# A two-layer encoder in split fp32: another lead-in, and weight splits held back at the heads of three feed-forwards

## The chip, the cores and the metric

The kernel runs on one core of one Trainium2 chip. The metric is device microseconds of that core from launch to end. Three runs of the kernel before took 1055.67, 1056.27 and 1058.92 us; the median, 1056.27, is the time before. Its engines are named as in the profile: PE (TensorE, matrix products), with PEld its weight loads, DVE (VectorE), ACT (ScalarE), POOL (GpSimd), and SP, whose queue issues the DMAs.

## The reference

x is 256 rows of 1024, float32. Two layers; each is a SwiGLU feed-forward with half weight, a mixer (a convolution module in the first layer, differential attention in the second), and another feed-forward. Each of these six sub-layers has a norm ahead and a norm behind:

```python
def _rmsnorm(x, g, eps=RMS_EPS):
    y = xf * lax.rsqrt(jnp.mean(xf * xf, axis=-1, keepdims=True) + eps)
    return (y * g.astype(jnp.float32)).astype(x.dtype)

def _half_ffn(x, g_pre, g_post, w_gate, w_up, w_down):
    h = _rmsnorm(x, g_pre)                      # w_gate, w_up: 1024 x 2816
    f = (jax.nn.silu(h @ w_gate) * (h @ w_up)) @ w_down
    return x + 0.5 * _rmsnorm(f, g_post)
```

## The kernel before

The six sub-layers are called a (feed-forward), b (convolution), c and d (feed-forwards), e (attention), f (feed-forward), and run in this order (the loop over `subs`, L762).

Products in float32 precision are made of three: every operand is split into a high part (rounded, `wh`, `xTh`, `hh`) and a low part (`wl`, `xTl`, `hl`: the operand less its high part), and `mm3` (L151) adds high x high, high x low and low x high in PSUM. So each weight is loaded as float32 (`raw`), ACT copies its high part (L113) and DVE subtracts for the low part (L114). The weights are jobs of 512 KB (128 partitions x 1024 numbers). There are 5 buffers for raw jobs and NW = 12 for split ones. `pump` (L119) issues load and split of the next jobs as long as fewer than 12 are ahead of the oldest not yet freed; `free` (L128) frees one and calls `pump`.

The 256 rows of x are two blocks of 128 (tb = 0, 1). `prenorm` (L181) squares a block on ACT (the tiles j), takes the mean and the power -1/2 on POOL, multiplies x by the gain and the norm on DVE (the tiles xn). `turn` (L209) then transposes the block on PE (the tiles pt) into xTh and xTl. `postnorm` (L219) does the like for the result of a sub-layer and adds it to x.

A feed-forward (`ffn`, L329) has 11 chunks of 256 columns of gate and up. A chunk of gate is two jobs (k 0 to 3 and 4 to 7 of the eight 128-row pieces), and so is one of up. The first two chunks (the lead) are done with x as the stationary operand (`proj_x`, L254): four tiles px, one for each block and chunk, each of 48 products with 256 columns, then silu on ACT (sx), the product on DVE (hx), and transposes of it on PE into the tiles ht (`flip`, L201; `hook_flips`, L205). So a tile can start before the second block is normed. In a the order of the tiles is `TURN` (both blocks of chunk 0, then of chunk 1), in c, d and f it is `TWO` (both chunks of block 0 first). From chunk 2 on, the main loop (`projs`, L273) makes the transposed result directly, 18 tiles gu, each with silu (sg), product (h) and split (hh, hl). `Down` (L287) adds the down products into four PSUM banks, that of tile kt after the gate and up products of tile kt + 1; those of the last 8 come at the end (`finish`, L315), block by block, so that the postnorm of block 0 lies beside the products of block 1.

Within an engine instructions run in the order that the scheduler of the framework sets. `tc.keep_in_program_order` and `after` (L73) fix it in places. All DMAs of the kernel are issued by SP, in order.

Of the kernel before, what the change touches and what calls it, by code (L numbers as in the profile page):

```python
# [35 lines left out]
NRAW = 5  # L36
NDV = 4
WARM = (16, 6, 6)


class _Side:
# [8 lines left out]
def trunk_kernel(  # L50
# [37 lines left out]
    warm = cp.tile([P, 1], F32, name="warm")  # L88
    ones_r = cp.tile([33, P], F32R, name="ones_r")
    A.activation(ones_r, ones_d[0:33, :], AF.Copy, scale=float(D))  # L90
    ones_e = cp.tile([P, 1], F32, name="ones_e")
    G.memset(ones_e, 1.0 / P)

# [10 lines left out]

    ready = {}

    def issue(i):
        src, shape = jobs[i]
        raw = rawp.tile([P, *shape], F32, tag="raw", name=f"raw{i}")
        nc.sync.dma_start(raw, src)  # L110
        hi = wp.tile([P, *shape], F32R, tag="wh", name=f"wh{i}")
        lo = wp.tile([P, *shape], F32R, tag="wl", name=f"wl{i}")
        A.copy(hi, raw)  # L113
        V.tensor_tensor(lo, raw, r32(hi), ALU.subtract)  # L114
        ready[i] = (hi, lo)

    issued, oldest, gone = [0], [0], set()

    def pump():  # L119
        while issued[0] < min(oldest[0] + NW, len(jobs)):  # L120
            issue(issued[0])
            issued[0] += 1

    def need(i):
        pump()
# [67 lines left out]
        pending.append(lambda: turn(tb, xn, name))  # L193

    pending, flips = [], []

    def hook():
        while pending:
# [55 lines left out]
    def proj_x(pairs, order, name):  # L254

        for n, (tb, i) in enumerate(order):
# [13 lines left out]
                hook()  # L270
            yield tb, i, ps

    def projs(pairs, name):  # L273

        for c, (w1, w2) in pairs:
            for f in range(2):
                ps = proj(w1, w2, f, f"{name}{2 * c + f}")
                if f:
                    w1.free()
                    w2.free()  # L280
                yield 2 * c + f, ps

    def split_to(hi, lo, src):
        A.copy(hi, src)
        V.tensor_tensor(lo, src, r32(hi), ALU.subtract)

    class Down:  # L287

# [35 lines left out]
                self.ws[kt].free()  # L324

    TWO = [(tb, i) for tb in range(NTB) for i in range(2)]
    TURN = [(tb, i) for i in range(2) for tb in range(NTB)]

    def ffn(hp, jb, name):  # L329
        dn = Down([w for r in jb for w in r[2]], TAIL, name)  # L330
        q = []

        def tiles(c):
# [6 lines left out]
        for tb, i, ps in proj_x([r[:2] for r in jb[:2]], TURN if name == "a" else TWO, name):  # L340
            sg = sp.tile([P, FC], F32, tag="sg", name=f"sx{name}{tb}{i}")
            A.activation(sg, ps[:, :FC], AF.Silu)
            h = sp.tile([P, FC], F32, tag="hf", name=f"hx{name}{tb}{i}")
            V.tensor_tensor(h, ps[:, FC:], sg, ALU.mult)
            for f in range(2):
                flip(turned[i][:, f, tb, :], h[:, f * P:(f + 1) * P])
        for kt, ps in projs([(c, jb[c][:2]) for c in range(2, len(jb))], name):
# [7 lines left out]
            A.activation(sg, ps[:, 0, :], AF.Silu)  # L355
# [272 lines left out]
    def attn(hp, name):  # L628
# [112 lines left out]


    subs = [
        ("a", lambda p: ffn(p, J00, "a"), ffn_norm_pre[0, 0], ffn_norm_post[0, 0], True, conv_params),
        ("b", lambda p: conv(p, "b"), mix_norm_pre[0], mix_norm_post[0], False, None),
        ("c", lambda p: ffn(p, J01, "c"), ffn_norm_pre[0, 1], ffn_norm_post[0, 1], True, None),
        ("d", lambda p: ffn(p, J10, "d"), ffn_norm_pre[1, 0], ffn_norm_post[1, 0], True, attn_params),
        ("e", lambda p: attn(p, "e"), mix_norm_pre[1], mix_norm_post[1], False, None),
        ("f", lambda p: ffn(p, J11, "f"), ffn_norm_pre[1, 1], ffn_norm_post[1, 1], True, None),
    ]  # L750
    nc.sync.dma_start(xs[0], x[0, 0:P, :])
    g = gain(subs[0][2], "prea")
    for n in range(2):
        issue(issued[0])
        issued[0] += 1
    nc.sync.dma_start(xs[1], x[0, P:S, :])
    with tc.high_priority():
        prenorm(0, g, "a")
        hook()
    prenorm(1, g, "a")  # L760
    for n, (name, body, _, post, half, also) in enumerate(subs):
        last = n == len(subs) - 1  # L762
        with tc.tile_pool(name=f"hp{name}", bufs=8) as hp:
            dn = body(hp)
            if also is not None:
                also()
            gpost = gain(post, f"post{name}")
            gpre = None if last else gain(subs[n + 1][2], f"pre{n + 1}")
            for tb in range(NTB):
                dn.finish(tb)  # L770
                with tc.high_priority():
                    postnorm(tb, dn.acc[tb], gpost, half, name, out[0] if last else None)
                    if not last:
                        prenorm(tb, gpre, subs[n + 1][0])
            dn.free()


# [29 lines left out]
```

## Time and profile before

| | |
|---|---|
| median of three runs | 1056.27 us |
| the profiled execution | 1059.09 us, its span 1057.4 us |
| PE busy | 1022.3 us, 97% |
| DVE, ACT, POOL busy | 659.4, 553.7, 72.4 us |
| mean granted clock of PE | 0.993 |
| read from HBM | 175.40 MB, 167 GB/s over the span |

The span runs from the first to the last instruction. A timeline's row has the start and the length of an instruction, or of several of one kind; in brackets stands how long the engine had been idle and what ended that. Products of PE overlap: a row of 0.28 us whose successor starts 0.12 us later took PE 0.12. The granted clock is in shares of 2.4 GHz; at the very start its column shows 1.00 while the products stand as far apart as at the lower level, so there the spacing is what to read.

### The profile page before, as it was taken

Reading aid. Unit: us, or ns where it says so; the run is one execution under the profiler, and the core shown is the slowest. Engines: PE = TensorE matmul, PEld = TensorE weight load, DVE = VectorE, ACT = ScalarE, POOL = GpSimd, SP = SyncE. Lnnn points to the kernel's source line nnn. Section 1 sums busy time; section 2 is a strip of 40 time slices with the busy share of each in tenths; the row PEclk is TensorE's granted clock in tenths of the full one; section 3 lists DMA queues with packets and bytes.
Section 4 is the critical chain, followed back from the end, with each engine's and each line's share of the span. In section 5 each row is a group of like instructions: output and inputs, shape, how many; then the busy total and the mean of one; then the engine's idle time right before and its main releaser. Section 6 shows DMA issues by size and latency. Waiting matters only on the chain.

```text
span 1057.4 us, 17903 instructions
## 1 busy us (share of the span) xinstructions
PE 1022.3 (97%) x7133; PEld 947.2 (90%) x7133; DVE 659.4 (62%) x1007; ACT 553.7 (52%) x933; POOL 72.4 (7%) x110
## 2 busy tenths in 40 slices
PE   6999999999979999999999999999999999999997
PEld 5999999899967989999989999998899789999995
DVE  6755556689996755545475555566778685555542
ACT  6564445476845644434455444454578665445431
POOL 1000000031460100000010000001001110000000
PEclk9999999999989999999999999999999999999999
DMA  9866465386000666465555564653843255664511
GB/s 297 284 210 223 152 199 181 111 267 197 4 1 1 226 205 223 149 215 180 160 181 178 182 224 153 199 182 125 283 148 101 80 168 185 191 215 158 185 58 40
DMA packets 130493, 177.62 MB, mean 168 GB/s; under 512 B 6174, under 2 KB 112710, under 8 KB 130409
## 3 DMA queue, kind: packets, MB, share of 16 engines
q1 hardware_dynamic: 130408, 176.47, 51.6%
q8 instruction: 56, 0.92, 0.3%
q14 instruction: 29, 0.23, 0.1%
HBM read 175.40 MB, written 1.05 MB: 167 GB/s over the span
## 4 chain that ended last, share of the span: by engine, by line
PE 78%; DVE 10%; DMA 4%; ACT 3%; issue 3%; POOL 2%; SPq 0%; DVEq 0%; POOLq 0%; ACTq 0%
DVE co L487 4%; PE gua L152 3%; PE gua L154 3%; PE gua L153 3%; PE guf L152 3%; PE guc L152 3%; PE guf L154 3%; PE guc L154 3%; PE gud L154 3%; PE guc L153 3%; PE gud L152 3%; PE gud L153 3%; PE guf L153 3%; DVE wl L114 2%; DMA raw<-in_ffn_w_gate_dram 2%
## 5 line engine op out<-in xcount | busy, mean ns | idle before, releaser
L114 DVE TENSOR_TENSOR wl<-raw,wh 128x1024 fp32r<-128x1024 f32 x320 | 389.1, 1223 | 134.4 <-ACT wh L113 132.1
L113 ACT CAST wh<-raw 128x1024 fp32r<-128x1024 f32 x320 | 333.7, 1051 | 137.5 <-PE accd L154 14.2
L152 PE MATMUL guf<-xTh,wh 128*128 128x256 f32 x288 | 82.1, 285 | 0.0
L152 PE MATMUL guc<-xTh,wh 128*128 128x256 f32 x288 | 82.1, 285 | 0.0
L152 PE MATMUL gua<-xTh,wh 128*128 128x256 f32 x288 | 82.1, 285 | 0.0
L154 PE MATMUL gua<-xTh,wl 128*128 128x256 f32 x288 | 81.7, 284 | 0.0
L154 PE MATMUL guf<-xTh,wl 128*128 128x256 f32 x288 | 81.7, 284 | 0.0
L154 PE MATMUL guc<-xTh,wl 128*128 128x256 f32 x288 | 81.7, 284 | 0.0
L152 PE MATMUL gud<-xTh,wh 128*128 128x256 f32 x288 | 81.2, 282 | 0.0
L154 PE MATMUL gud<-xTh,wl 128*128 128x256 f32 x288 | 81.1, 281 | 0.0
L153 PE MATMUL gud<-xTl,wh 128*128 128x256 f32 x288 | 81.1, 281 | 0.0
L153 PE MATMUL guc<-xTl,wh 128*128 128x256 f32 x288 | 81.0, 281 | 0.0
L153 PE MATMUL gua<-xTl,wh 128*128 128x256 f32 x288 | 81.0, 281 | 0.0
L153 PE MATMUL guf<-xTl,wh 128*128 128x256 f32 x288 | 81.0, 281 | 0.0
L487 DVE SCALAR_TENSOR_TENSOR co<-u,wdw,co 128x256 f32<-128x256 f32 x120 | 61.7, 578 | 0.0
L153 PEld LDWEIGHTS guc<-xTl,wh 128*128 128x128 f32 x288 | 54.7, 190 | 0.5
L153 PEld LDWEIGHTS guf<-xTl,wh 128*128 128x128 f32 x288 | 54.6, 190 | 0.5
L153 PEld LDWEIGHTS gua<-xTl,wh 128*128 128x128 f32 x288 | 54.6, 190 | 0.5
L152 PEld LDWEIGHTS guf<-xTh,wh 128*128 128x128 f32 x288 | 54.4, 189 | 0.5
L152 PEld LDWEIGHTS gua<-xTh,wh 128*128 128x128 f32 x288 | 54.4, 189 | 0.5
L152 PEld LDWEIGHTS guc<-xTh,wh 128*128 128x128 f32 x288 | 54.4, 189 | 0.5
L152 PEld LDWEIGHTS gud<-xTh,wh 128*128 128x128 f32 x288 | 54.2, 188 | 0.5
(357 smaller groups left out, 2670.3 us busy)
## 6 DMA issues: line engine op xcount, KB each, us to landing
raw<-in_ffn_w_gate_dram SPq DMA_DIRECT2D x88, 512.0 KB, 5.0
raw<-in_ffn_w_up_dram SPq DMA_DIRECT2D x88, 512.0 KB, 4.8
raw<-in_ffn_w_down_dram SPq DMA_DIRECT2D x88, 512.0 KB, 4.7
raw<-in_conv_w_pw_dram SPq DMA_DIRECT2D x24, 512.0 KB, 4.7
raw<-in_attn_w_qkv_dram SPq DMA_DIRECT2D x24, 512.0 KB, 4.8
raw<-in_attn_w_o_dram SPq DMA_DIRECT2D x8, 512.0 KB, 4.6
gpre<-in_ffn_norm_pre_dram SPq DMA_DIRECT2D x3, 512.0 KB
x<-in_x_dram SPq DMA_DIRECT2D x2, 512.0 KB
```

The lines of the kernel that those rows point to most:

```text
L113: A.copy(hi, raw)
L114: V.tensor_tensor(lo, raw, r32(hi), ALU.subtract)
L152: T.matmul(o, sh, mh, start=first, stop=False)
L153: T.matmul(o, sh, ml, start=False, stop=False)
L154: T.matmul(o, sl, mh, start=False, stop=last)
L487: tap[ct, t] = V.scalar_tensor_tensor(c, u[:, t:t + S], wdw[:, ct, t:t + 1], c, ALU.mult, ALU.add)
```

## The change

In the lead-in, `first_norm` replaces the broadcast load of the gain, the two `prenorm` and the two `turn` of a. It loads the gain as 8 rows of 128 and transposes it, transposes raw x, multiplies by the gain per partition out of PSUM (ya), and splits that into xTh and xTl. The norm rs, one number a row of x, is worked out later and applied to the products: as the scale of silu and a factor in the lead, and as two multiplications by `row` (rs along the columns) in the 18 tiles of the main loop of a. 24 products of 32 rows run on PE ahead of x (`WARM0`). A load of x or a weight waits for the last load but one (`in_turn`); the first six weights are split at places written out by hand.

`proj_jobs` does the lead of a weight by weight: both blocks of a tile for one job, then the next; in each the products with low x come before those with low weights. The second chunk's two tiles lie in banks of the down sums (`acc`). The second block of x is turned inside the first twelve products.

In c, d and f `hold` limits the jobs that may be issued to the first 8 of the feed-forward. `release` lets two more after the second tile, two after the third and all after the fourth, each behind the silu and product of that tile on ACT and DVE. The parameter loads are issued after the 17th weight load.

```diff
-    def issue(i):
-        src, shape = jobs[i]
-        raw = rawp.tile([P, *shape], F32, tag="raw", name=f"raw{i}")
-        nc.sync.dma_start(raw, src)
...
     def pump():
-        while issued[0] < min(oldest[0] + NW, len(jobs)):
-            issue(issued[0])
-            issued[0] += 1
+        while issued[0] < min(oldest[0] + NW, limit[0]):
+            i, raw, _ = fetch()
+            split_to(*slot(i), raw)
+
+    def hold(first, n=None):
+        limit[0] = len(jobs) if n is None else first + n
+
+    def release(upto, *done):
+        with ExitStack() as st:
+            for ins in done:
+                st.enter_context(after(ins))
+            limit[0] = len(jobs) if upto is None else upto
+            pump()
...
+    def first_norm(row):
...
+        for _ in range(WARM0):
+            for g in range(4):
+                q = slice(32 * g, 32 * g + 32)
+                pin(T.matmul(four[g][:, 0:S], ident_r[q, :], twice[q].to_broadcast([32, 2, P]),
+                             start=True, stop=True))
...
+            d = pin(nc.sync.dma_start(dst, src)) if dst is not None else pin(fetch_into(w))
+            if len(last) > 1:
+                tc.add_manual_dep(d.ins, last[-2].ins.name, mybir.DependencyInfo(
+                    mybir.DependencyClass.Sync, mybir.DependencyReason.DATA), reason="in_turn")
+            last.append(d)
...
+        pin(nc.sync.dma_start(gr, row.rearrange("(k p) -> k p", p=P)))
+        get(xs[0], x[0, 0:P, :])
+        get(None, None)
+        get(xs[1], x[0, P:S, :])
+        for _ in range(3):
+            get(None, None)
...
+        turned(0, 0, ps_acc, "acc")
+        turned(0, 1, ps_acc, "acc")
+        scaled(0, 0)
+        weight_high(0)
+        high(0, 0)
+        scaled(0, 1)
+        high(0, 1)
+        low(0, 0)
+        weight_low(0)
+        weight_high(1)
+
+        def second():
+            turned(1, 0, ps_mi, "mi")
+            scaled(1, 0)
+            high(1, 0)
+            low(0, 1)
+            low(1, 0)
+            weight_low(1)
+            weight_high(2)
...
+    def proj_jobs(pairs, name):
...
+                        for n, (s, v) in enumerate(((xTh, 0), (xTl, 0), (xTh, 1))):
+                            if first and n == 2:
+                                pending.pop(0)()
+                            for k in range(k0, k0 + w.per):
+                                pin(T.matmul(ps[:, m * FC:(m + 1) * FC], s[:, k, c], w(k)[v],
+                                             start=n + k == 0, stop=n == 2 and k == KD - 1))
...
+                r = late[:, tb:tb + 1]
+                sa = A.activation(sg, ps[:, :FC], AF.Silu, scale=r)
+                hv = V.scalar_tensor_tensor(h, ps[:, FC:], r, sg, ALU.mult, ALU.mult)
             for f in range(2):
                 flip(turned[i][:, f, tb, :], h[:, f * P:(f + 1) * P])
+            release((j0 + LEAD, j0 + LEAD + 2, j0 + LEAD + 4, None)[n] if late is None else
+                    (j0 + 6, j0 + 10, j0 + 12, None)[n], sa, hv)
...
+                V.tensor_tensor(sg, ps[:, 0, :], row, ALU.mult)
+                A.activation(sg, sg, AF.Silu)
+                V.tensor_tensor(sg, sg, row, ALU.mult)
...
-        prenorm(0, g, "a")
-        hook()
-    prenorm(1, g, "a")
+        late = first_norm(subs[0][2])
+    heads = [None] + [jb[0][0].ids[0] for jb in (J01, J10)] + [None, J11[0][0].ids[0]]
...
+            with after(fetched[LATER]):
+                if also is not None:
+                    also()
...
+            if not last:
+                if heads[n] is None:
+                    release(None)
+                else:
+                    hold(heads[n], LEAD)
             dn.free()
```

What stands where on three engines follows. In the names a number behind the letters is the job (wh0), the block and half (xnd10: block 1, half 0) or the block and chunk (pxd01).

On ACT at the start, before: the squares (ja) of block 0, two weights, then the copies of transposed x.

```order
L186 ACTIVATE ja00_123,ppa0_122<-x0_95 128x512
L186 ACTIVATE ja01_127,ppa0_122<-x0_95 128x512
L113 CAST wh0_111<-raw0_109 128x1024
L113 CAST wh1_117<-raw1_115 128x1024
L216 CAST xTh_97<-pta00_137 128x4x128
L186 ACTIVATE ja10_152,ppa1_151<-x1_96 128x512
L216 CAST xTh_97<-pta01_144 128x4x128
L186 ACTIVATE ja11_156,ppa1_151<-x1_96 128x512
L113 CAST wh2_178<-raw2_176 128x1024
```

After: the first weight stands ahead of the copies of x, each further weight ahead of a copy of the second block, and the squares come behind all of them.

```order
L95 CAST ident_r_93<-ident_79 128x128
L285 CAST wh0_167<-raw0_139 128x1024
L275 CAST xTh_99<-ya00_165 128x4x128
L275 CAST xTh_99<-ya01_171 128x4x128
L285 CAST wh1_176<-raw1_142 128x1024
L275 CAST xTh_99<-ya10_199 128x4x128
L285 CAST wh2_205<-raw2_144 128x1024
L275 CAST xTh_99<-ya11_217 128x4x128
L282 ACTIVATE ja00_222,parts0_152<-x0_97 128x512
```

The squares moved from the front to behind the fourth copy of x, and the copies wait for ya, not for the normed x.

On DVE at the head of d, where block 1 is normed, before:

```order
L114 TENSOR_TENSOR wl164_5962<-raw164_5959,wh164_5961 128x1024
L231 SCALAR_TENSOR_TENSOR x1_96<-ync10_5906,rsqc1_5916,x1_96 128x512
L231 SCALAR_TENSOR_TENSOR x1_96<-ync11_5910,rsqc1_5916,x1_96 128x512
L188 TENSOR_TENSOR xnd10_5923<-x1_96,gpre3_5763 128x512
L188 TENSOR_TENSOR xnd11_5927<-x1_96,gpre3_5763 128x512
L114 TENSOR_TENSOR wl165_5968<-raw165_5965,wh165_5967 128x1024
L161 TENSOR_SCALAR mspd1_5929<-ppd1_5920 128x1
L114 TENSOR_TENSOR wl166_5974<-raw166_5971,wh166_5973 128x1024
L192 TENSOR_SCALAR xnd10_5923<-xnd10_5923,rspd1_5931 128x512
L192 TENSOR_SCALAR xnd11_5927<-xnd11_5927,rspd1_5931 128x512
L114 TENSOR_TENSOR wl167_5980<-raw167_5977,wh167_5979 128x1024
L344 TENSOR_TENSOR hxd00_6044<-pxd00_5993,sxd00_6042 128x256
```

The jobs 164 to 167 are the ninth to twelfth of d. After, the same stretch:

```order
L370 SCALAR_TENSOR_TENSOR x1_98<-ync10_5972,rsqc1_5982,x1_98 128x512
L370 SCALAR_TENSOR_TENSOR x1_98<-ync11_5976,rsqc1_5982,x1_98 128x512
L210 TENSOR_TENSOR xnd10_5989<-x1_98,gpre3_5829 128x512
L210 TENSOR_TENSOR xnd11_5993<-x1_98,gpre3_5829 128x512
L183 TENSOR_SCALAR mspd1_5995<-ppd1_5986 128x1
L214 TENSOR_SCALAR xnd10_5989<-xnd10_5989,rspd1_5997 128x512
L214 TENSOR_SCALAR xnd11_5993<-xnd11_5993,rspd1_5997 128x512
L509 TENSOR_TENSOR hxd00_6081<-pxd00_6031,sxd00_6080 128x256
L356 TENSOR_TENSOR xTl_100<-ptd10_6120,xTh_99 128x4x128
L356 TENSOR_TENSOR xTl_100<-ptd11_6127,xTh_99 128x4x128
L509 TENSOR_TENSOR hxd01_6150<-pxd01_6084,sxd01_6149 128x256
L448 TENSOR_TENSOR wl164_6156<-raw164_6153,wh164_6155 128x1024
```

The four subtractions wl164 to wl167 moved from between the steps of the norm to behind hxd01, or later.

On PE in the second tile of d, before, where the transposes of the first hx (htd0) and of block 1 (ptd10) stand:

```order
L154 MATMUL pxd01_6046<-wh163_5955,xTl_98 128x256
L152 MATMUL pxd01_6046<-wh163_5955,xTh_97 128x256
L207 MATMUL htd0_5991<-ident_79,hxd00_6044 128x128 x2
L213 MATMUL ptd10_6082<-ident_79,xnd10_5923 128x128 x4
L153 MATMUL pxd01_6046<-wl163_5956,xTh_97 128x256
L154 MATMUL pxd01_6046<-wh163_5955,xTl_98 128x256
```

After:

```order
L176 MATMUL pxd01_6084<-wh161_6009,xTl_100 128x256
L346 MATMUL htd0_6029<-ident_79,hxd00_6081 128x128 x2
L174 MATMUL pxd01_6084<-wh162_6015,xTh_99 128x256
L175 MATMUL pxd01_6084<-wl162_6016,xTh_99 128x256
L176 MATMUL pxd01_6084<-wh162_6015,xTl_100 128x256
```

The transposes of hx moved from behind the 40th to behind the 24th product of that tile; those of block 1 come nine products later.

## Rows read from the trace of the kernel before

**Rows 1.** The page, busy time of each engine, its share of the span, instructions.
```profile
PE 1022.3 (97%) x7133; PEld 947.2 (90%) x7133; DVE 659.4 (62%) x1007; ACT 553.7 (52%) x933; POOL 72.4 (7%) x110
```

**Rows 2.** Waits of PE, by what ended them: us, times, longest.
```profile
PE htd L207 <- DVE hxd L344: 2.7, 2, 2.4
PE hta L207 <- DVE hxa L344: 1.4, 1, 1.4
...
PE htc L207 <- DVE hxc L344: 1.2, 2, 0.9
PE htf L207 <- DVE hxf L344: 1.1, 2, 1.0
```

**Rows 3.** Timeline of the lead-in: start, length, engine, line, what, count [idle before].
```profile
0.80 0.38 SPq L751 DMA_DIRECT2D x<-in_x_dram  x1
...
4.50 0.63 ACT L186 ACTIVATE ja<-x 128x512 bf16<-128x512 f32 x1 [2.10 <-DMA x<-in_x_dram]
...
8.21 1.05 ACT L113 CAST wh<-raw 128x1024 fp32r<-128x1024 f32 x1 [2.23 <-DMA raw<-in_ffn_w_gate_dram]
...
8.37 1.97 PE L213 MATMUL pta<-ident,xna 128*128 128x128 f32 x8 [8.37 <-DVE xna L192]
...
9.70 1.05 ACT L113 CAST wh<-raw 128x1024 fp32r<-128x1024 f32 x1 [0.45 <-DMA raw<-in_ffn_w_gate_dram]
...
11.29 0.58 PE L152 MATMUL pxa<-wh,xTh 128*128 128x256 f32 x1 [0.95 <-ACT xTh L216]
```

**Rows 4.** Timeline of PE, products three apart, in the lead-in and main loop.
```profile
13.68 0.41 PE L152 MATMUL pxa<-wh,xTh 128*128 128x256 f32 x1
...
14.32 0.41 PE L152 MATMUL pxa<-wh,xTh 128*128 128x256 f32 x1
...
41.15 0.28 PE L152 MATMUL gua<-xTh,wh 128*128 128x256 f32 x1
...
41.50 0.28 PE L152 MATMUL gua<-xTh,wh 128*128 128x256 f32 x1
```

**Rows 5.** Timeline of PE, scores of the attention, two row groups in a row.
```profile
771.61 0.28 PE L671 MATMUL sc<-ql,qh 64*128 64x256 f32 x2
771.73 0.28 PE L671 MATMUL sc<-qh,ql 64*128 64x256 f32 x2
```

**Rows 6.** The page, DMA issues: KB each, us from issue to landing.
```profile
raw<-in_ffn_w_gate_dram SPq DMA_DIRECT2D x88, 512.0 KB, 5.0
```

**Rows 7.** Groups of DVE and of ACT, 0 to 60 us: busy, mean ns.
```profile
L114 DVE TENSOR_TENSOR wl<-raw,wh 128x1024 fp32r<-128x1024 f32 x24 | 28.7, 1222 | 11.5 <-ACT wh L113 11.5
L217 DVE TENSOR_TENSOR xTl<-pta,xTh 128x512 fp32r<-128x512 f32 x4 | 2.7, 684 | 0.2 <-ACT xTh L216 0.2
...
L216 ACT CAST xTh<-pta 128x512 fp32r<-128x512 f32 x4 | 2.3, 581 | 2.1 <-PE pta L213 2.1
```

**Rows 8.** Timeline of the head of d, DVE, ACT, POOL and PE.
```profile
544.54 1.41 DVE L231 SCALAR_TENSOR_TENSOR x<-ync,rsqc,x 128x512 f32<-128x512 f32 x2 [0.43 <-POOL rsqc L163]
...
547.27 1.05 ACT L113 CAST wh<-raw 128x1024 fp32r<-128x1024 f32 x1 [2.45 <-DMA raw<-in_ffn_w_up_dram]
...
548.23 0.63 ACT L186 ACTIVATE jd<-x 128x512 bf16<-128x512 f32 x1
...
550.09 1.39 POOL L163 TENSOR_TENSOR rspd<-mspd,nhalf 128x1 f32<-128x1 f32 x1 [5.59 <-DVE mspd L161]
...
551.51 0.88 DVE L192 TENSOR_SCALAR xnd<-xnd,rspd 128x512 f32<-128x512 f32 x2 [0.43 <-POOL rspd L163]
...
553.92 0.69 PE L207 MATMUL htd<-ident,hxd 128*128 128x128 f32 x2 [2.38 <-DVE hxd L344]
```

**Rows 9.** Stretch of the head of d: busy by engine, granted clock, DMA.
```profile
553.90:557.30 3.40, 3.38 (x16) 3.38 (x17) 0.69 (x1) 0.68 (x2) 0.00 (x0) 0.50 0.65 211
```

**Rows 10.** Tile gua, its readers: count, ns min/median/max, first and last start.
```profile
L355 ACT ACTIVATE sga<-gua x18: 372/384/387, 47.3 to 185.1; 128x256 f32<-128x256 f32 x18
L357 DVE TENSOR_TENSOR hfa<-gua,sga x18: 414/423/425, 47.7 to 186.5; 128x256 f32<-128x256 f32 x18
```

More of the change, by code (lines that the diff above doesn't have):

```diff
@@ L105, in trunk_kernel, with fetch, slot @@
     ready = {}
-    def issue(i):
+    issued, oldest, gone = [0], [0], set()
+    fetched = []
+    def fetch():
+        i = issued[0]
+        issued[0] += 1
         src, shape = jobs[i]
         raw = rawp.tile([P, *shape], F32, tag="raw", name=f"raw{i}")
-        nc.sync.dma_start(raw, src)
[L111 to L117, printed above, removed]
-    def pump():
-        while issued[0] < min(oldest[0] + NW, len(jobs)):
-            issue(issued[0])
-            issued[0] += 1
+        fetched.append(nc.sync.dma_start(raw, src))
+        return i, raw, fetched[-1]
+    def slot(i):
+        ready[i] = [wp.tile([P, *jobs[i][1]], F32R, tag=t, name=f"{t}{i}") for t in ("wh", "wl")]
+        return ready[i]
+    limit = [0]
+    def pump():
+        while issued[0] < min(oldest[0] + NW, limit[0]):
[9 more added lines that the diff above has]
+            pump()
     def need(i):
@@ L271, in proj_x @@
             yield tb, i, ps
+    def proj_jobs(pairs, name):
+        pin = tc.keep_in_program_order
+        for i, pair in enumerate(pairs):
+            pool, tag = ((ps_gu, "gu"), (ps_acc, "acc"))[i]
+            banks = [pool.tile([P, 2 * FC], F32, tag=tag, name=f"px{name}{tb}{i}") for tb in range(NTB)]
+            for m, w in enumerate(pair):
+                for k0 in range(0, KD, w.per):
+                    for tb, ps in enumerate(banks):
+                        c = slice(tb * P, (tb + 1) * P)
+                        first = (i, m, k0, tb) == (0, 0, 0, 0)
+                        for n, (s, v) in enumerate(((xTh, 0), (xTl, 0), (xTh, 1))):
[4 more added lines that the diff above has]
+                                             start=n + k == 0, stop=n == 2 and k == KD - 1))
+                        if first:
+                            pending.pop(0)()
+                        elif (m, k0, tb) == (0, w.per, 0):
+                            hook_flips()
+                w.free()
+            for tb, ps in enumerate(banks):
+                yield tb, i, ps
     def projs(pairs, name):
@@ L353, in ffn @@
                     put(i, hi, lo)
-            sg = sp.tile([P, S], F32, tag="sg", name=f"sg{name}{kt}")
-            A.activation(sg, ps[:, 0, :], AF.Silu)
+                if late is not None:
+                    pr = ps_mi.tile([P, S], F32, tag="mi", name=f"pr{name}")
+                    for tb in range(NTB):
+                        T.transpose(pr[:, tb * P:(tb + 1) * P], late[:, tb:tb + 1].to_broadcast([P, P]), ident)
+                    row = hp.tile([P, S], F32, name="row", bufs=1)
+                    A.copy(row, pr)
+            sg = sp.tile([P, S], F32, tag="sg", name=f"sg{name}{kt}")
+            if row is None:
+                A.activation(sg, ps[:, 0, :], AF.Silu)
+            else:
+                V.tensor_tensor(sg, ps[:, 0, :], row, ALU.mult)
+                A.activation(sg, sg, AF.Silu)
+                V.tensor_tensor(sg, sg, row, ALU.mult)
             h = sp.tile([P, S], F32, tag="hf", name=f"hf{name}{kt}")
@@ L764, in trunk_kernel @@
             dn = body(hp)
[L765 to L768, printed above, removed]
+            with after(fetched[LATER]):
+                if also is not None:
+                    also()
+                gpost = gain(post, f"post{name}")
+                gpre = None if last else gain(subs[n + 1][2], f"pre{n + 1}")
             for tb in range(NTB):
```

93 lines of the change are left out of this document (78 added, 15 removed).

## The prediction

> **What bounds the kernel now.** I read the engine totals first. TensorE (PE) is busy 97% of the span [rows 1], so what can be had is where it waits or runs slowly, and work taken off another engine counts only there. The waits of PE, summed by what ended them, come next [rows 2]: those of the transposes called ht, at the head of each feed-forward, are 2.7 us in sub-layer d, 1.4 in a, 1.2 in c and 1.1 in f.
>
> Then the lead-in in order of time [rows 3]. The first half of x is used at 4.50, but PE's first transpose starts at 8.37, its longest wait, since the transposes take x already multiplied by gain and norm. The first product starts at 11.29. PE is then at half speed: three products take 0.64 us from 13.68 to 14.32, against 0.35 from 41.15 to 41.50, which is 213 ns a product against 119 [rows 4]: 256 columns at 1.2 and at 2.4 GHz. The first product of the main loop (gua) starts at 41.15 [rows 4]. The four tiles between are 4 x 48 products, 22.8 us at 119 ns, yet take 29.9.
>
> Last, the head of d [rows 8]. The second block's x is updated from 544.54, two operations of 0.71 to 545.95. The sums of its squares (jd) start only at 548.23, because a weight split (wh) that waits for its DMA until 547.27 is ahead of them in ACT's queue. The norm follows at 550.09, the scaling at 551.51; one more weight split stands between it and the gate product hxd, for which PE's transposes wait until 553.92, after 2.38 us of idle. In the 3.40 us after that the granted clock is 0.50 [rows 9]: another 1.7 us lost.
>
> **The lead-in, step by step.** Raw x is transposed, so the first transposes wait for x alone. A DMA of 4 KB (gr) is issued ahead of x, some 0.4 us like other issues [rows 3], so x0 is there at 4.9. The gain's broadcast copy of 512 KB goes.
>
> On ACT the first weight's split now stands ahead of the x splits. That weight is now second instead of third among the large loads; in the trace the first two weights come 1.5 us apart, 8.21 and 9.70 [rows 3], so it lands near 6.4. Then wh0 ends at 7.45 (1.05 us [rows 3]) and the first high part of x at 8.1 (0.58 [rows 7]). The first product starts at 8.1 instead of 11.29.
>
> From there PE waits for DVE and ACT. The second x may be issued only when the first has landed. With the 3.7 us from issue to use of x [rows 3] it lands at 8.6, the next weights at 10.1, 12.4 and 13.9. ACT takes wh1 before the x of the second block: 10.2 to 11.3, then xTh10 to 11.9. DVE (0.68 for a half of x, 1.22 for a weight [rows 7]) has xTl00 at 8.8, wl0 10.0, ya10 10.7, xTl01 11.4, xTl10 12.6, wl1 13.9, ya11 14.6, xTl11 15.9, wl2 17.2, wl3 18.4.
>
> A weight and a block are 12 products, 1.43 us at full speed. Block 2 of weight 0 can start at 12.0, block 2 of weight 1 at 15.2 (it ends near 16.9); the other four fill 5.7 us, to 22.6. The second pair is 11.4 us and its four transposes 0.3, which puts gua at 34.3. If the half speed lasts until 16, block 2 of weight 1 ends near 18.5 and gua is at 35.9. I take the middle, 35.1: 6.0 us before 41.15. The transposes inside the first gua tile need hxa of the last lead tile, which two weight splits precede on both queues: 0.4 us back. Lead-in: 5.6 us.
>
> The loads are the uncertain part. The median from issue to landing under load is 5.0 us [rows 6]; with two in flight that is a load each 2.5 us. Then x1 lands at 9.9, the weights at 11.4, 15.0 and 16.5, block 2 of weight 1 ends at 18.5, and gua is near 35.9, or 37 with the slow clock: still 4 us of gain.
>
> The Trainium skill, "DMA: Bandwidth & Descriptors", section "Anatomy of one DMA", gives 2.0 us plus the bytes over 436 GB/s for one transfer (for its software-issued path): an estimate of 3.2 us for 512 KB. It speaks for the shorter figure, and by it the lead-in gains 0.3 us more than by the 3.7 us.
>
> The row of products for warming (24 of 32 rows each, in four row groups) runs before x is there only if the groups run together. The scores of the attention, 64 rows in two groups, show it: each pair is one row, and the pairs start 0.12 us apart, the time of one product [rows 5]. Six times four at half speed are then 1.3 us, done by about 4.5. One after another they would be 24 x 0.213 = 5.1 us; the transposes of x would start near 7.7 instead of 4.9, the chain from there some 2 us later, and the lead-in would gain 3.6 us.
>
> The Trainium skill, "TensorEngine Tiling (Array Packing)", section "Theoretical Speedup", allows up to four at a time for 32 rows; the rows agree for two, and no run here shows four yet.
>
> **What a pays later.** Two transposes of the norm add 0.3 us to PE. Each of the 18 tiles of the main loop of a gets two more DVE multiplications, about 0.42 each [rows 10]. They lie beside PE's next product of 48 x 0.119 = 5.7 us: 0.42 + 0.38 + 0.42 + 0.42, and two weight splits of 1.22 between them, are 4.1 us. Cost 0; from below it is 0 too, from above 2 us, should a few tiles come late. The later loads of the convolution's parameters, the moved allocation of the sums and the small copies are hidden likewise.
>
> **The heads of c, d, f.** Eight weight splits stood in DVE's and ACT's queues through the postnorm and norm of the second block; now four do, and none stands behind the postnorm's start. In d the squares then follow x: the first runs beside x's second update, the second from 546.0 for 0.63 and a short readout, to 546.8. On DVE the two products with the gain (0.68 each) end near 547.3 and the mean's 0.2 behind them; POOL 547.6 to 549.0 (1.39), scaling 0.88 to 549.9, hxd (0.42) at 550.3, where before it was 553.9 [rows 8]. But PE's order moves too: the transposes stand after 24 products of the second tile, not after 40, so PE gets there 16 x 0.119 = 1.9 us earlier: 553.92 - 2.38 - 1.9 = 549.6. 0.7 us of wait stay, less than d's 2.38 that cost the clock, and less than c's longest of 0.9 [rows 2]. d: 2.7 + 1.7 - 0.7 = 3.7 us.
>
> In c and f the waits are 1.2 and 1.1 [rows 2], and the same 0.7 should stay: 0.5 and 0.4, bounds 0 and 1.2. Heads: 4.6 us, bounds 2 and 6.5 (all waits and the clock gone).
>
> The held splits come back after the fourth tile. Of the down weights, the first is split 1.1 + 1.2 us after the last hx, the main loop's first tile gives it 5.7; the sixth must wait for a raw buffer and its load, and stands ahead of the low half of hh that the third down product needs. With 5.0 us from issue to landing [rows 6] that is some 0.7 us in time. Cost 0, up to 2 us in each of three.
>
> **The sum.** 5.6 - 0.3 + 4.6 = 9.9 us. Against the profiled execution, 1059.09 (span 1057.4 and 1.7 around it), that is 1049.2. That execution lies 2.8 above the median 1056.27, and the runs reach from 1055.67 to 1058.92; I set the gain against the median: 1046.4.
>
> **Rivals.**
> - The lead gives only 3 to 4 us (loads near 5 us, the warming row by row, or a late clock): 1048 to 1050.
> - The heads gain nothing, since what is held back is missed at the third down product, some 1.5 us in each of c, d and f: 1056.3 - 5.3 = 1051.0. For it speaks how close that split is; against it, that 0.7 us in time is my estimate and that a split which comes late once need not come late in all three.
> - The change doesn't do what it says: the lead is bound by the weights' loads, not by the norm, and both places gain under 3.2 us: 1054 to 1057. Against it, PE needs 2.85 us for each weight of the pairs and a load takes 1.5 to 2.5.
> - Slower: in a the gate's chain has become four links. Tiles 14 to 21 stand back to back, with two product banks, so a tile can start only when the last but one is out of its bank. If splits that wait for a weight buffer, freed only by the running product, stand between the links, each such tile slips. It decides from 5.7 us after a tile's last product; I reckon 3 to 4. At 2 us in seven tiles it costs 14: 1060.6.
>
> **Chances.** The forecast 0.62, small lead 0.14, heads without gain 0.08, nothing done 0.08, slower 0.08. A difference of 0.3% (3.2 us) is about what can be told here. Faster by more: 0.62 + 0.14 + 0.08, less a little for the edges, 0.83; same 0.09; slower 0.08. The forecast's own bounds are 4 to 7.5 for the lead and 2 to 6.5 for the heads, less 0 to 2: 1042 to 1052. With the small lead and half of the third case I give 1041.5 to 1053.
>
> **What would show it.** First product of pxa near 8 us, gua at 34 to 37; no wait ahead of hta; waits of htc, htd and htf of 0.5 to 1 us and a granted clock of 1.00 through the head of d; the squares of d right behind x. It is wrong if gua is later than 38, if PE waits for hh or a product bank in a, or if accd waits for the low part of hh.

## The result and the profile after

| | median us | runs | lowest to highest |
|---|---|---|---|
| before | 1057.68 | 5 | 1055.67 to 1059.98 |
| changed | 1045.25 | 5 | 1044.16 to 1046.06 |

The ratio is 0.9883 (95% interval 0.9866 to 0.9899): 12.4 us faster, where 9.9 was forecast; 1045.25 lies in the range given. The two profiled executions differ by 13.9 us of span (1057.4 and 1043.5); that of before took 1059.09, 1.4 above its median.

Where they came, by the first product of each stage (us from the start of the span, from the groups by tile of both traces; `gained` is what a row adds to the one above):

| first product of | before | changed | earlier by | gained |
|---|---|---|---|---|
| lead of a (pxa) | 11.29 | 7.99 | 3.3 | 3.3 |
| main loop of a (gua) | 41.15 | 34.79 | 6.4 | 3.1 |
| lead of c (pxc) | 348.0 | 342.2 | 5.8 | -0.6 |
| sums of c (accc) | 380.5 | 372.5 | 8.0 | 2.2 |
| lead of d (pxd) | 540.9 | 532.9 | 8.0 | 0.0 |
| sums of d (accd) | 576.0 | 563.2 | 12.8 | 4.8 |
| lead of f (pxf) | 858.5 | 846.8 | 11.7 | -1.1 |
| sums of f (accf) | 891.0 | 877.2 | 13.8 | 2.1 |

So in this pair the lead-in gave 5.8 us net (forecast 5.3), the heads of c, d and f 9.1 (forecast 4.6), and 1.1 went back, 0.86 in d's main loop and 0.26 in the attention.

The engine totals: PE has 1.1 us less busy time than in [rows 1], and the span is 13.9 shorter, so on balance what went is waiting. Busy time itself fell by 2.2 us in the lead of d, where the slow stretch is gone, and rose by the row of 24 (1.66) and by d's main loop (0.9).

```profile
PE 1021.2 (98%) x7160; PEld 947.3 (91%) x7160; DVE 669.1 (64%) x1039; ACT 550.9 (53%) x933; POOL 66.0 (6%) x109
```

The waits of PE, by what ended them (us in total, times, longest). None of the four of [rows 2] is left, none is for hh, for a weight or for a product bank of a.

```profile
PE pv L753 <- DVE sum L748: 6.0, 1, 6.0
PE warm L229 <- ACT ident_r L95: 2.6, 1, 2.6
...
PE pte L352 <- DVE xne L214: 1.1, 1, 1.1
...
PE pxa L427 <- ACT xTh L275: 1.0, 1, 1.0
```

The lead-in in order of time, against [rows 3, 4]. The row of 24 (warm) takes 1.66 us, x is turned from 5.08 (8.37 before), and the first product comes at 7.99, behind the split of the first weight and the first high part of x, as the forecast had it (7.45 and 8.1). In the changed kernel products are 0.12 to 0.13 us apart, full speed, from 12.73 on (the second of the four that begin at 12.35); four take 0.47 us from 13.66. Before, they were 0.21 apart until 18.10, so full speed too comes 5 us earlier.

```profile
1.26 0.36 SPq L236 DMA_DIRECT2D x<-in_x_dram  x1
...
2.64 1.66 PE L229 MATMUL warm<-ident_r 32*128 32x256 f32 x24 [2.64 <-ACT ident_r L95]
...
5.08 1.94 PE L264 MATMUL pta<-ident,x 128*128 128x128 f32 x8 [0.45 <-DMA x<-in_x_dram]
...
6.37 1.04 ACT L285 CAST wh<-raw 128x1024 fp32r<-128x1024 f32 x1 [3.78 <-DMA raw<-in_ffn_w_gate_dram]
...
7.99 1.22 PE L427 MATMUL pxa<-wh,xTh 128*128 128x256 f32 x4 [0.97 <-ACT xTh L275]
...
10.53 1.04 ACT L285 CAST wh<-raw 128x1024 fp32r<-128x1024 f32 x1 [2.08 <-DMA raw<-in_ffn_w_gate_dram]
...
12.35 0.91 PE L427 MATMUL pxa<-wh,xTh 128*128 128x256 f32 x4
...
13.66 0.64 PE L427 MATMUL pxa<-wl,xTh 128*128 128x256 f32 x4
14.13 0.63 PE L427 MATMUL pxa<-wh,xTh 128*128 128x256 f32 x4
...
34.79 0.28 PE L174 MATMUL gua<-xTh,wh 128*128 128x256 f32 x1
```

The end of half speed before:

```profile
17.95 0.32 PE L154 MATMUL pxa<-wh,xTl 128*128 128x256 f32 x1
18.10 0.28 PE L152 MATMUL pxa<-wh,xTh 128*128 128x256 f32 x1
```

The head of d, against [rows 8, 9]: the squares follow the first update of x by 0.85 us, POOL's power takes 0.54 us and not 1.39, hxd ends at 540.3, and the transposes come at 541.41 without a wait, at granted clock 1.00.

```profile
535.64 1.42 DVE L370 SCALAR_TENSOR_TENSOR x<-ync,rsqc,x 128x512 f32<-128x512 f32 x2 [0.72 <-POOL rsqc L185]
536.49 0.63 ACT L208 ACTIVATE jd<-x 128x512 bf16<-128x512 f32 x1 [2.67 <-DVE x L370]
...
538.53 0.55 POOL L185 TENSOR_TENSOR rspd<-mspd,nhalf 128x1 f32<-128x1 f32 x1 [2.92 <-DVE mspd L183]
...
539.91 0.41 DVE L509 TENSOR_TENSOR hxd<-pxd,sxd 128x256 f32<-128x256 f32 x1
...
541.41 0.38 PE L346 MATMUL htd<-ident,hxd 128*128 128x128 f32 x2
```
```profile
541.40:544.80 3.40, 3.40 (x31) 3.33 (x30) 0.69 (x1) 0.59 (x1) 0.00 (x0) 1.00 0.10 40
```

The longer chain of a: at tile 15 the last reader of the bank, hfa, ends at 146.95, 3.1 us after the tile's last product, and the bank is next written by the product at 149.47, 2.5 us later. Over the 18 tiles hfa ends 1.8 to 4.0 us behind (the first two, behind the lead, 8.8 and 4.7), and the bank is wanted 2.5 us or more after that.

```profile
146.53 0.42 DVE L540 TENSOR_TENSOR hfa<-gua,sga 128x256 f32<-128x256 f32 x1
...
149.47 0.28 PE L174 MATMUL gua<-xTh,wh 128*128 128x256 f32 x1
```

### The profile page after: what moved, and what is told of

Same layout as the page of the kernel before. It is cut to its first block, busy times and chain, and to the rows that moved or that the text cites. A ratio compares the mean times of both kernels' runs of the same rounds, so it can differ in the third digit from the quotient of the medians.

```text
span 1043.5 us, 17937 instructions
## 1 busy us (share of the span) xinstructions
PE 1021.2 (98%) x7160; PEld 947.3 (91%) x7160; DVE 669.1 (64%) x1039; ACT 550.9 (53%) x933; POOL 66.0 (6%) x109
## 4 chain that ended last, share of the span: by engine, by line
PE 89%; DVE 6%; ACT 2%; POOL 1%; DMA 1%; issue 1%; SPq 0%; DVEq 0%; POOLq 0%; ACTq 0%
DVE co L670 4%; PE gud L175 3%; PE guf L176 3%; PE gud L176 3%; PE guc L176 3%; PE gua L176 3%; PE guf L175 3%; PE guc L175 3%; PE gua L175 3%; PE gua L174 3%; PE guc L174 3%; PE guf L174 3%; PE gud L174 3%; PE pxa L427 2%; PE acca L174 2%; PE accc L174 2%
## 5 line engine op out<-in xcount | busy, mean ns | idle before, releaser
L448 DVE TENSOR_TENSOR wl<-raw,wh 128x1024 fp32r<-128x1024 f32 x314 | 380.1, 1223 | 102.8 <-ACT wh L448 99.9
L448 ACT CAST wh<-raw 128x1024 fp32r<-128x1024 f32 x314 | 325.3, 1050 | 106.4 <-PE gua L175 11.6
L175 PEld LDWEIGHTS gud<-xTl,wh 128*128 128x128 f32 x288 | 54.1, 188 | 0.5
```

Source lines behind the costliest of these rows:

```text
L175: T.matmul(o, sh, ml, start=False, stop=False)
L448: return A.copy(hi, src), V.tensor_tensor(lo, src, r32(hi), ALU.subtract)
```

## The experiments

Ratios are to the kernel before, run on the same chip, with their 95% intervals; the changed kernel has 0.9883 (0.9866 to 0.9899).

**One part alone.** The lead-in alone (nothing held):

```diff
-            release((j0 + LEAD, j0 + LEAD + 2, j0 + LEAD + 4, None)[n] if late is None else
+            release(None if late is None else
                     (j0 + 6, j0 + 10, j0 + 12, None)[n], sa, hv)
...
-    heads = [None] + [jb[0][0].ids[0] for jb in (J01, J10)] + [None, J11[0][0].ids[0]]
+    heads = [None] * 5
```

> The new lead-in alone; nothing is held back at the heads of c, d and f. Theory (the two parts add up, as the two traces split them: first gua product 6.35 us earlier, 0.45 of it back by the end of a, so some 5.8 from the lead-in and some 8.1 from the rest): 1051.9 us beside 1057.7 of before, first gua product at 34.8 us, the waits of PE for hxc, hxd and hxf back at 1.2, 2.7 and 1.1 us, POOL's power in these heads at 1.4 us. Rival (my forecast's split: the heads give 4.6 and the lead-in the rest): 1049.9. Second rival (the earlier lead-in shifts what falls together in the heads, so their waits go by themselves): near 1046, no waits for hxc, hxd, hxf.

The holds alone. The old lead-in is put back (`late = None`), and the parameter loads no longer wait for the 17th weight load:

```diff
-        for n, (tb, i, ps) in enumerate(proj_jobs(lead, name) if late is not None else proj_x(lead, TWO, name)):
+        for n, (tb, i, ps) in enumerate(proj_jobs(lead, name) if late is not None else proj_x(lead, TURN if name == "a" else TWO, name)):
...
+    late = None
+    nc.sync.dma_start(xs[0], x[0, 0:P, :])
+    g = gain(subs[0][2], "prea")
...
     with tc.high_priority():
-        late = first_norm(subs[0][2])
+        prenorm(0, g, "a")
+        hook()
+    prenorm(1, g, "a")
...
-            with after(fetched[LATER]):
+            with nullcontext():
```

> The lead-in of before; the splits held back at the heads of c, d and f. Theory (parts add up): 1049.6 us, first gua product at 41.15, no wait of PE for hxc, hxd or hxf, POOL's power 0.54 us there. Rival (my forecast's split): 1053.1. If 1052 or more with the waits gone, what is held back is paid for later, and a wait of PE for hh or a weight shows up in c, d or f.

Measured: lead-in alone 1053.24 us, ratio 0.9948 (0.9930 to 0.9965), 5.5 us; holds alone 1050.71, ratio 0.9928 (0.9914 to 0.9943), 7.6 us. The parts add up (13.1 for 12.4), and the forecast's split does not hold: it gave the heads 4.6 us, and their interval alone is 6.0 to 9.1. The waits of PE with the lead-in alone:

```profile
PE htf L346 <- DVE hxf L509: 1.9, 1, 1.9
PE htc L346 <- DVE hxc L509: 1.8, 2, 1.5
...
PE htd L346 <- DVE hxd L509: 0.8, 1, 0.8
```

They are back, but not as expected: longer in c and f, in d shorter and without a slow clock. The three leads take 33.2, 32.3 and 33.3 us to the first product of the sums, for 32.5, 35.1 and 32.5 before and 30.3 to 30.4 with the holds in either kernel. The 2.4 us stop of d was thus partly the timing of that program; the other five heads with the splits in them lose 2 to 3 us each. With the holds alone only a's own wait is left of that kind:

```profile
PE hta L344 <- DVE hxa L508: 1.4, 1, 1.4
```

Its time shows less than the 9.1 us of the table. In its trace the leads are 9.2 us shorter too, but b is 1.6 us longer than before (PE waits 2.8 us for the tiles dg, for 1.7) and d's main loop 0.9. What made b longer, no run shows.

**POOL's power beside a DVE operation.** The forecast took POOL's 1.39 us from [rows 8] as its duration. In the trace before, each of the 11 powers on 128x1 that take 1.38 us or more starts 0.16 to 0.23 us behind the start of a weight split on DVE, and ends 0.4 us behind that split. The other 13 take 0.54 to 0.56: DVE is idle beside 12 of them, and the one at 6.38 starts 0.24 us ahead of a DVE operation. In the postnorm of d's head, before:

```profile
542.89 1.22 DVE L114 TENSOR_TENSOR wl<-raw,wh 128x1024 fp32r<-128x1024 f32 x1
...
543.12 1.38 POOL L163 TENSOR_TENSOR rsqc<-msqc,nhalf 128x1 f32<-128x1 f32 x1 [8.37 <-DVE msqc L161]
```

To test it, one operation that nobody reads was put beside four of them (`mi` is the mean ahead of it on DVE; `BESIDE` names the postnorm and the norm of the second block at the heads of d and f):

```diff
+    BESIDE = ("qc1", "pd1", "qe1", "pf1")
...
-        V.tensor_scalar(ms, parts[:, 0:1], parts[:, 1:2], eps, ALU.add, ALU.add)
+        mi = V.tensor_scalar(ms, parts[:, 0:1], parts[:, 1:2], eps, ALU.add, ALU.add)
...
+        if name in BESIDE:
+            with after(mi):
+                V.tensor_tensor(beside[0], xs[0], xs[0], ALU.subtract)
         power[0] = G.tensor_tensor(rs, ms, nhalf[:, 0:1], ALU.pow)
```

> The changed kernel with one DVE subtraction of 128x1024 on data that nothing reads, put behind the mean of the postnorm and of the prenorm of the second block at the heads of d and f (four in all). Theory (POOL's power on 128x1 lasts until the DVE operation beside it ends): it takes 1.4 instead of 0.54 us in these four places, the gate product hxd ends 1.7 us later (542.0 for 540.3), PE's transposes wait 0.6 to 0.7 us in d and about 0.5 in f; time up by 1 to 2 us. Rival (POOL was slow in the kernel before for another reason, its DMAs or semaphores): 0.54 us as before, DVE's own order delays hxd by 0.9 only, the transposes do not wait, time unchanged.

Measured: 1046.86 us, ratio 0.9889 (0.9872 to 0.9907): by the time not told apart from the changed kernel, but the rows decide. All four take 1.38 to 1.46 us and end 0.4 us behind the DVE operation; in the changed kernel the same four take 0.54 to 0.55. The transposes wait 0.5 us in d and in f.

```profile
539.16 1.22 DVE L188 TENSOR_TENSOR beside<-x 128x1024 f32<-128x1024 f32 x1
539.39 1.39 POOL L189 TENSOR_TENSOR rspd<-mspd,nhalf 128x1 f32<-128x1 f32 x1 [2.93 <-DVE mspd L184]
540.81 0.88 DVE L218 TENSOR_SCALAR xnd<-xnd,rspd 128x512 f32<-128x512 f32 x2 [0.44 <-POOL rspd L189]
```
```profile
PE htf L350 <- DVE hxf L513: 0.5, 1, 0.5
...
PE htd L350 <- DVE hxd L513: 0.5, 1, 0.5
```

The Trainium skill, "SBUF — State Buffer", section "Who interferes with whom", says that a DVE instruction with two SBUF inputs contends with a GpSimd instruction that reads SBUF, and that whichever issues first holds the shared ports for its whole length. This case agrees: 0.54 us alone, 1.39 where a DVE subtraction of 1.22 had started first, 0.56 where POOL had started first.

**How many splits may stay.** Four more are let through in each head:

```diff
-LEAD = 8
+LEAD = 12
```

> The changed kernel with four more splits let through at the heads of c, d and f (LEAD 12 for 8): four weight splits stand again between the postnorm and the gate product hx on DVE, and four on ACT. Theory (these splits, and POOL's power beside them, were the wait): POOL's power is at 1.4 us again, hx 4 to 5 us later, which is more than the 1.1 us by which it is early now, so PE's transposes wait 1 to 3 us in c, d and f and the time is 1049 to 1053. Rival (only what stands behind a late DMA matters, so four ready splits cost little): waits under 0.5 us each, time within 1.5 us of 1045.3.

Measured: 1050.89 us, ratio 0.9929 (0.9916 to 0.9941), so some 5 us of the gain (0.0046 of 1058) are gone. PE waits about 1 us in each head again, POOL's power in d is slow, and the three leads take 31.9, 31.9 and 32.2 us, 5.0 more in sum than in the changed kernel. The splits in the queue were the wait.

```profile
536.75 1.39 POOL L185 TENSOR_TENSOR rsqc<-msqc,nhalf 128x1 f32<-128x1 f32 x1 [8.35 <-DVE msqc L183]
```
```profile
PE htf L346 <- DVE hxf L509: 1.2, 1, 1.2
...
PE htc L346 <- DVE hxc L509: 0.9, 1, 0.9
PE htd L346 <- DVE hxd L509: 0.8, 1, 0.8
```

**Parts of the lead-in.** The row of 24 products, left out:

```diff
-WARM0 = 6
+WARM0 = 0
```

> The changed kernel without the row of 24 products ahead of x. Theory (the row brings PE's full speed forward): products in the lead-in stay 0.21 us apart beyond 12.7 us, to 15 or so, and the first gua product comes about 1 us later, near 35.8; time 1046 to 1047. Rival (the full speed comes from the continuous work behind it): spacing and the first gua product as now, within 0.2 us; time unchanged, 1045.

Measured: 1045.08 us, ratio 0.9873 (0.9855 to 0.9890). Products are at full speed from 12.63 on (12.73 with the row), the first gua product is at 34.8. The row does nothing for the clock here: in the other traces with the row and the new lead-in it comes between 12.6 and 14.1.

```profile
12.41 0.73 PE L427 MATMUL pxa<-wh,xTh 128*128 128x256 f32 x4
```

Loads that do not take turns:

```diff
-            if len(last) > 1:
+            if len(last) > 99:
```

> The changed kernel without the rule that a load of the lead-in is issued only when the last but one has landed: x0, the first weight, x1 and three more weights are issued one behind the other; no instruction moves on any engine. Theory (loads in flight share the DMAs, so each of the first ones lands later): the first weight is split near 8 us (8.21 in the kernel before, 6.37 now), the first product of pxa comes at 9 to 9.5 for 7.99, the first gua product some 1 us later than 34.8; time 1046. Rival (the later ones land earlier and PE waits for these, not for the first): first product late, but gua at 34.8 or before; time unchanged or 0.5 us less.

Measured: 1045.41 us, ratio 0.9879 (0.9866 to 0.9893); gua at 35.0. Both guesses fell: six loads in flight do not delay the first weight (split at 6.33 for 6.37), and gua does not come earlier although the second weight does, by 1.0 us (9.52 for 10.53). In this trace half speed also lasts longer, to 14.0; but in the last run below the loads do not take turns either, full speed comes at 12.8, and gua is at 34.7.

```profile
6.33 1.05 ACT L285 CAST wh<-raw 128x1024 fp32r<-128x1024 f32 x1 [3.74 <-DMA raw<-in_ffn_w_gate_dram]
...
9.52 1.05 ACT L285 CAST wh<-raw 128x1024 fp32r<-128x1024 f32 x1 [1.10 <-DMA raw<-in_ffn_w_gate_dram]
...
12.31 1.22 PE L427 MATMUL pxa<-wh,xTh 128*128 128x256 f32 x4
```

A second weight that lands later does show. Its split starts at 10.53 in the changed kernel (gua at 34.79); at 11.13 with the operations beside POOL's powers gua is at 35.15, and at 11.26 with the lead-in alone at 35.30. Nothing in these two edits bears on that load, so these are differences between executions.

```profile
11.26 1.05 ACT L285 CAST wh<-raw 128x1024 fp32r<-128x1024 f32 x1 [2.64 <-DMA raw<-in_ffn_w_gate_dram]
```

The second pair in the banks of the first:

```diff
-            pool, tag = ((ps_gu, "gu"), (ps_acc, "acc"))[i]
+            pool, tag = ((ps_gu, "gu"), (ps_gu, "gu"))[i]
```

> The changed kernel with the second column pair of a's lead in the two banks of the first pair instead of two of its own; no instruction moves. Theory: its first product (22.9 us now) must wait until hxa has read the first pair's bank (24.4 us now): PE stands 1.5 us there, gua comes at 36.3; time 1046.8. If PE then runs at half speed behind the wait, up to 2 us more. Rival (hidden, since the first pair's banks are read in time): no wait, gua at 34.8, time unchanged.

Measured: 1046.71 us, ratio 0.9891 (0.9876 to 0.9906), by the time not told apart from the changed kernel; gua at 36.7, 1.9 us later. There are two new stops of 1.0. Only the one for hxa, ahead of the second pair, is a wait for a bank; it costs 1.1 us. The other, for xTh, stands in the first pair and comes from the second weight, whose split starts at 11.32 in this trace, 0.8 us later. So the banks are worth some 1.1 us of the 1.9.

```profile
11.32 1.05 ACT L285 CAST wh<-raw 128x1024 fp32r<-128x1024 f32 x1 [2.82 <-DMA raw<-in_ffn_w_gate_dram]
...
12.94 0.73 PE L427 MATMUL pxa<-wh,xTh 128*128 128x256 f32 x4 [1.03 <-ACT xTh L275]
...
24.75 0.73 PE L427 MATMUL pxa<-wh,xTh 128*128 128x256 f32 x4 [0.99 <-DVE hxa L513]
```

The lead's products block by block (a pair's weights are then freed behind both blocks):

```diff
-            for m, w in enumerate(pair):
-                for k0 in range(0, KD, w.per):
-                    for tb, ps in enumerate(banks):
+            for tb, ps in enumerate(banks):
+                for m, w in enumerate(pair):
+                    for k0 in range(0, KD, w.per):
```

> The changed kernel with the lead's products of a in the order of before within a pair: all 48 of the first block, then all 48 of the second, instead of 12 and 12 for each weight as it lands. Theory (what the lead-in gains past the first product is that two blocks of products cover each load and split): the first block waits for each low half of a weight in turn (ready at 9.8, 14.2, 17.2 and 18.4 us now), ends at 19.3, the second takes 5.7 more, gua comes at 37 instead of 34.8; time 1047.4, more if the waits keep PE at half speed. Rival (the earlier first product is all the gain): gua at 34.8, time unchanged.

Measured: 1047.34 us, ratio 0.9907 (0.9895 to 0.9920); gua at 37.3, 2.5 us later, with the waits on the low halves (the second weight's split starts late here too, at 11.19, which by the two executions above is some 0.4 of it):

```profile
PE pxa L427 <- DVE wl L289: 2.4, 2, 1.4
```

So of the 6.4 us to gua, some 2 hang on the order of the products and some 1.1 on the banks, each left out alone, and none on the row or the turns.

**The chain of a**, six links for four:

```diff
-                V.tensor_tensor(sg, ps[:, 0, :], row, ALU.mult)
+                for _ in range(3):
+                    V.tensor_tensor(sg, ps[:, 0, :], row, ALU.mult)
```

> The changed kernel with two more multiplications in each of the 18 main tiles of a (the one that reads the gate from its bank is done three times, with the same outcome), so that the chain that empties a bank has six links. PE's order is unchanged. Theory (the last reader of a bank, hfa, ends 1.8 to 3.1 us after the tile's last product now and the bank is wanted 2.5 us or more later still): hfa some 0.8 to 2 us later, no wait of PE, time 1045.3. Rival (the slower case of my forecast): PE waits for hfa at some of the tiles 15 to 21, 1 us or more each, time 1048 to 1055.

Measured: 1045.92 us, ratio 0.9895 (0.9880 to 0.9909), and no wait of PE for hfa or sga. The 54 reads take 424 ns each. But the chain grows by more than the 0.85 us of the two added links, since weight splits get between them: where the tiles stand back to back hfa now ends up to 5.5 us behind a tile's last product, and the bank is wanted as little as 0.09 us after that. That fits the forecast's slower case, which begins 5.7 us behind a tile: four links are 2.5 us away from it, six stand at its edge, and no run went past it.

```profile
154.78 0.42 DVE L541 TENSOR_TENSOR hfa<-gua,sga 128x256 f32<-128x256 f32 x1
...
155.29 0.35 PE L174 MATMUL gua<-xTh,wh 128*128 128x256 f32 x1
```
```profile
L537 DVE TENSOR_TENSOR sga<-gua,row x54: 413/424/425, 46.4 to 181.9; 128x256 f32<-128x256 f32 x54
```

**Holding ahead of the attention too.** In the changed kernel POOL's power still takes 1.39 us at the head of e, and PE waits 1.1 us for xne.

```diff
-    heads = [None] + [jb[0][0].ids[0] for jb in (J01, J10)] + [None, J11[0][0].ids[0]]
+    heads = [None] + [jb[0][0].ids[0] for jb in (J01, J10)] + [JV[0].ids[0], J11[0][0].ids[0]]
...
-                split_to(vh[:, tb, HALF[n]], vl[:, tb, HALF[n]], pv)
+                release((first + LEAD, first + LEAD, first + LEAD + 4, None)[2 * tb + n],
+                        *split_to(vh[:, tb, HALF[n]], vl[:, tb, HALF[n]], pv))
```

Here `first` is `JV[0].ids[0]`.

> The changed kernel with the same hold ahead of the attention (e): only the eight splits of the values' weights go ahead, the rest come back behind the value tiles. Theory: POOL's power at the head of e falls from 1.39 to 0.54 us, the wait of the transposes pte for xne (1.1 us) goes, the time is 1.0 to 1.5 us less: 1044. Rival (the first query and key weights then come late): a wait of 1 to 3 us for a weight at the first tile of queries, time 1045 to 1047.

Measured: 1046.89 us, ratio 0.9892 (0.9879 to 0.9906). The wait for xne is gone, but the DMAs then stand still (share 0.01 from 735 to 745), the splits come back beside the first softmax, and PE waits there. From the first value product to the first product of f, e takes 125.8 us; in the 11 traces without a hold in e it takes 122.5 to 123.8 (123.2 in the changed kernel).

```profile
735.00:745.00 10.00, 10.00 (x45) 8.10 (x44) 3.63 (x5) 4.40 (x6) 0.00 (x0) 1.00 0.01 2
```
```profile
PE at L885 <- DVE tt L878: 2.1, 1, 2.1
```

With the release behind the second value tile (`(first + LEAD, None, None, None)`):

> The changed kernel with the hold ahead of the attention, and everything let go behind the second value tile instead of the last. Theory (the hold itself saves the 1.1 us wait for xne, and what it cost came from splits that returned beside the first softmax): head of e 1.5 us shorter as with the longer hold, no wait of 2.1 us for tt, time 1043.8, the fastest so far. Rival (whatever is held in e comes back beside the softmax): a wait for tt of 1 to 2 us again, time 1045.5 to 1047.

Measured: 1043.78 us, ratio 0.9878 (0.9864 to 0.9892). The DMAs run again in that stretch, the longest wait for tt is 0.5, and e takes 122.4 us.

```profile
735.00:745.00 10.00, 10.00 (x45) 8.11 (x44) 8.28 (x8) 7.77 (x9) 0.00 (x0) 1.00 0.56 167
```
```profile
PE at L885 <- DVE tt L878: 1.0, 3, 0.5
```

Last, the same without the row of 24 and without the turns:

> The kernel with the short hold ahead of the attention, without the row of 24 products ahead of x and without the rule that loads of the lead-in take turns, both of which made no difference when left out alone. Theory (they do nothing together either, and the hold ahead of e is worth 1 to 1.5 us again): first gua product at 34.8, PE does not wait for xne, 1043.8 us. Rival (one covers for the other: loads that share the DMAs need the earlier work of PE, or the reverse): gua after 35.5, 1044.8 or more.

Measured: 1044.76 us, ratio 0.9870 (0.9851 to 0.9888); gua at 34.7, e again 122.4. So what the long hold costs is clear in its trace, and the early release takes it away. That the short hold gains on no hold is not shown: 122.4 lies 0.1 us under the shortest e without one, the wait for xne that it removes is 0.5 to 1.4 us among those traces, and the intervals of both ratios overlap that of the changed kernel.

## Why the prediction was right, and where not

- **First product and gua**: right. 7.99 for 8.1, 34.79 for 35.1. The last two low halves of the first pair's weights were forecast for 17.2 and 18.4 and are ready at 17.3 and 18.4; the block order run shows that PE's waits for them matter. Half speed ended at 12.7, earlier than the 16 of the later bound. The 0.4 us that hxa was to give back were not paid: the last transposes of hxa follow the product ahead of them without a wait (37.63, behind 37.51).
- **The row of 24**: right that the four groups run together (24 products in 1.66 us, done by 4.3; forecast 4.5), wrong that it matters: without it nothing changes.
- **Loads**: between the two figures of the forecast. The first weight takes 4.7 us from issue to landing (1.67 to 6.35), the second block of x 3.5 (4.96 to 8.48). Earlier loads bring nothing (gua within 0.2 us with all in flight), a second weight 0.7 later costs 0.5. So the small-lead rival did not come, with what it feared seen at a small size.
- **What a pays**: right at 0 for the longer chain. hfa ends 1.8 to 4.0 us behind a tile, for 3 to 4 reckoned. From the first gua product to the first product of b, a takes 167.7 to 167.9 us in every kernel with the new lead-in and 167.3 to 167.4 with the old one: 0.4, for 0.3 forecast (besides the two transposes of the norm, two more of hxa stand in it). (The 1060.6 of the slower rival is 1046.4 + 14, so 1060.4; nothing hangs on it.)
- **The heads**: right in mechanism, too small: 4.6 for 9.1 in the traces and 7.6 (6.0 to 9.1) with the holds alone. Both lie above the forecast's upper bound of 6.5 (the interval of the second reaches down to 6.0), though that bound was to be all waits and the clock gone (6.7 by [rows 2] and the 1.7 of the slow stretch). The step that failed is "0.7 us of wait stay". It used POOL's 1.39 us and, for x, the 544.54 of before. Both hold a power beside a split; without the split each is 0.85 us shorter, so hxd ends 7.45 us after the first product of the lead and not 9.36, 1.1 before PE wants it. That is 0.7 in each of three heads, 2.1 of the 4.5 that were missing.
- The second cause, in c and f above all, is my reading of a wait: it is counted from the modelled end of the last product. Before, in c, the last product of 376.82 counts as busy for 0.28 and the next work starts at 377.42, a wait of 0.32; with its successor 0.12 behind, as elsewhere, 0.48 are lost. So each stop costs 0.16 us more than the view says. PE's idle time in the lead of c was 1.45 us over three stops (32.50 less 31.05 busy), one of them, of 0.2 for xTl, not counted in the forecast; 2.2 came back. The rest, some 0.3 us in c and in f, stays without a cause.

```profile
376.82 0.28 PE L154 MATMUL guc<-xTh,wl 128*128 128x256 f32 x1
377.42 0.44 PE L207 MATMUL htc<-ident,hxc 128*128 128x128 f32 x2 [0.32 <-DVE hxc L344]
```

- **Return of the held splits**: right at 0 in c, d and f. From the first sums on, c takes 160.4 us and f 166.3 to 166.4 in every trace, with or without holds. The long hold in e shows the case that was feared.
- **Luck**: the 1046.4 us forecast and the 1045.25 measured lie closer than the gains do, 9.9 and 12.4. The median of before was 1056.27 us when the forecast was made and 1057.68 beside the result, which hides 1.4 of the difference.
- Open: d's main loop, from the first sums to the first value product, is 0.9 us longer than before (160.4 for 159.5; products of gud 0.1198 us apart for 0.1186). It belongs to neither part by itself: all 13 other traces have 160.4, those with one part alone too. In the execution before, a, c and f have products 0.1198 apart as well, so its d is the odd one; whether that is this execution or this program, no run here tells.

## What to carry to other kernels

Before a duration is carried into the sum for the changed kernel, look at what ran beside it: a small operation that looks slow may be waiting for a neighbour, and goes fast when the change moves the neighbour away. What is held back must return before the DMAs run dry, and not beside the next chain that PE waits for. Where a longer chain makes nobody wait, read how much slack is left: here 2.5 us with four links and 0.09 with six. A part whose purpose is plain (a row for the clock, loads in turn) may still do nothing; leaving it out costs one run.

## What was not expected of the hardware

POOL's power on 128x1 takes 0.54 us, and 1.38 to 1.47 where a DVE subtraction of 128x1024 has started before it. And the granted clock does not show the slow products of the lead-in: it reads 1.00 from 14 to 15 us before, where products are 213 ns apart [rows 4], as at 1.2 GHz, while the slow stretch of [rows 9] reads 0.50. At the start of a program the spacing of the products has to be read.

```profile
14.00:15.00 1.00, 1.00 (x7) 1.00 (x7) 1.00 (x3) 0.97 (x1) 0.39 (x1) 1.00 1.10 348
```
